# Low parts of the attention's weight sets by ScalarE's negated high part and an accumulating DMA, and reordering copies that run in the order of what they write

## The chip, the cores and the metric

The kernel runs on one core of a Trainium2 chip. The time is device microseconds from launch to end; a run gives one number per execution, and the median of several is compared. In the profile PE is TensorE's matmul and PEld its weight load, DVE is VectorE, ACT is ScalarE, POOL is GpSimd, SP is SyncE, which here issues most of the DMAs.

## What is computed

A trunk of two encoder layers on 512 tokens of width 1024, in float32. Each layer projects x, runs two attentions on the projections (mixer A: windowed, with a learned sink; mixer B: three groups of heads with windows of stride 1, 4 and 16, mixed by their softmax denominators), projects and gates both branches, and ends with two layer norms and a squared-ReLU MLP. Cut to what matters here:

```python
def _mixer_sublayer(x, cos, sin, w_in, b_gate, a_sink, w_branch_a, w_branch_b, w_out):
    proj = jnp.einsum('bsd,de->bse', x, w_in)
    qa, ka, va, qb, kb, vb, gl = jnp.split(proj, IN_SPLITS, axis=-1)
    ...
    oa, _ = _banded_attention(qa, ka, va, A_WINDOW, a_sink)
    ya = jnp.einsum('bse,ed->bsd', oa.reshape(bsz, seq, A_Q_W), w_branch_a)
    ...
    for g, (window, dil) in enumerate(B_GROUPS):      # ((128, 1), (512, 4), (2048, 16))
        o, lse = _dilated_attention(qb[:, :, hs], kb[:, :, hs], vb[:, :, hs], window, dil)
    ...
    yb = jnp.einsum('bse,ed->bsd', ob.reshape(bsz, seq, B_OUT_W), w_branch_b)
    return jnp.einsum('bsd,de->bse', ga * ya + gb * yb, w_out)
```

## The kernel before

Float32 products are made from float32r parts: an operand w is split into a high part hi = round(w) and a low part lo = w − hi, and a product takes three matmuls, hi·hi, lo·hi and hi·lo (`mm3`, lines 279 to 281: the third is the first that reads the low part of the weights). The splits are work for other engines than PE.

Weights arrive in sets of 128 x 1024: `fetch` (L248, DMA from SP into "wst", three buffers) and `prep`, which splits the set into "whi" and "wlo" (three buffers each). `weights(key)` takes the next set of a plan and, with LOOK = 2, makes `prep` of the set two places ahead. So the cast of set c+2 runs as soon as PE has left set c−1, whose buffers it takes, and the set is wanted when PE begins c+2. There are two ways to split. `split` casts on ACT (L227) and subtracts on DVE (L228). `split_later` casts on ACT (L232), writes −hi into the low part on ACT (L233), and lets a DMA issued by POOL add w to it (L234). Which one a set gets is decided by its membership in the tuple LATER; before the change that is only ("ple", 1, 0) of layer 0 and ("start", 0) of layer 1. One activation operand, "pl", is made by `split_later` as well (three such splits in all, around 750 to 765 us).

The attention of a layer (`attention_block`) runs a list FLOW of projections (two "qa", eight "g" gates, and for two head pairs sp and three groups g the sets "qb", "kb", "vb"; four sets "ba" of the branch projection), 24 matmuls for each projection, and puts the attention units (scores, softmax, transposes, weighted sums) between them. The order on PE is made when the program is recorded: a class `Forecast` keeps estimated times of ACT, DVE and POOL, and a unit's next step is taken when the forecast says that its operands are there; otherwise a matmul of a projection goes in. The forecast charges each prep to ACT and DVE by fixed costs, before and after the change alike. The order on ACT, DVE, POOL and SP is set by a scheduler. On the chip each engine runs its list in order and waits where an operand is late. PSUM has one bank "o" for weighted sums; a join (L447 on ACT, L448 on DVE) has to empty it before the next begins.

For groups 1 and 2, tokens are sorted by residue class. `natural` and `sigma` are two views of the same 512 columns: the first in token order, the second in sorted order. `rope` writes the split q and k of these groups through `sigma` (the cast "qh" on L227, the subtraction "ql" on L228), and `values` copies v out of PSUM through it (L392).

Of the kernel before, what the change touches and what calls it, by code (L numbers as in the profile page):

```python
# [24 lines left out]
DEPTH = 2  # L25
# [3 lines left out]
LN_EPS = 1e-5  # L29
ROPE_THETA = 500000.0  # L30
NEG = -3.0e38
LATER = ((0, ("ple", 1, 0)), (1, ("start", 0)))
LOOK = 2
WARM = 11
FLOW = [("qa", 2), ("g", 0), ("qa", 3), ("g", 1), ("b", 0, 0), ("g", 2), ("b", 0, 1), ("b", 0, 2), ("g", 3),
# [165 lines left out]
def build(nc, tc, plan, down, xT, xN, pT, wst, vec, rows, sink, cst, out):  # L201
# [3 lines left out]
    with ctx:  # L205
# [4 lines left out]
        def bank(tag, name):  # L210
            return pp.tile([P, 512], F32, tag=tag, name=name, bufs={"mm": 3, "s": 2, "pt": 2, "o": 1}[tag])
# [14 lines left out]
        def split(hi, lo, src):  # L226
            nc.scalar.copy(hi, src)  # L227
            nc.vector.tensor_tensor(lo, src, hi.bitcast(F32), ALU.subtract)  # L228
# [22 lines left out]
        def prep(c):  # L251
# [3 lines left out]
            for a in cuts:  # L255
                (split_later if plan[c][0] in LATER else split)(hi[:, a], lo[:, a], st[:, a])
            ready[c] = (hi, lo)
# [90 lines left out]
        def attention_block(l, av, rp, vt, OA, OB, begun):  # L348
# [8 lines left out]
                if not l:  # L357
                    nc.sync.dma_start(ident, cst[:, off:])

            def natural(ap):  # L360
                return ap.rearrange("p (a b c) -> p a b c", a=32, b=4)

            def sigma(ap):
                return ap.rearrange("p (c b a) -> p a b c", c=4, b=4)

            def forecast_split(n, after):
                h = fc.on("act", 0.05 + n / 1200, after + HOP)
                return h, fc.on("dve", 0.07 + n / 960, h + HOP)

            def rope(ps, dil, name):  # L370
                sw = av.tile([P, S], F32, tag="sw", name="sw" + name, bufs=2)
                t1 = av.tile([P, S], F32, tag="t1", name="t1" + name, bufs=2)
                nc.vector.stream_shuffle(sw, ps, SWAP)
                nc.vector.tensor_tensor(t1, ps, cc["cos"], ALU.mult)
                nc.gpsimd.tensor_tensor(sw, sw, cc["sin"], ALU.mult)
                nc.vector.tensor_tensor(t1, t1, sw, ALU.add)
                hi = av.tile([P, S], F32R, tag="qh", name="qh" + name, bufs=5)
                lo = av.tile([P, S], F32R, tag="ql", name="ql" + name, bufs=5)
                if dil:
                    split(sigma(hi), sigma(lo), natural(t1))  # L380
                else:
                    split(hi, lo, t1)
                a = fc.on("dve", 0.6, fc.t + HOP)
                b = fc.on("dve", 0.6, a)
                c = fc.on("pool", 1.23, a + HOP)
                fc.give("mm", b + HOP)
                return hi, lo, forecast_split(S, fc.on("dve", 0.6, max(b, c) + HOP))[1] + HOP

            def values(ps, kind, name):
                v = av.tile([P, S], F32, tag="vT", name="vT" + name, bufs=2)  # L390
                if kind == "sigma":
                    nc.scalar.copy(sigma(v), natural(ps))  # L392
                elif kind == "edge":
                    nc.scalar.copy(v[:, 0:64], ps[:, 448:512])
                    nc.scalar.copy(v[:, 64:128], ps[:, 0:64])
                    nc.scalar.copy(v[:, 128:512], ps[:, 64:448])
                else:
                    nc.scalar.copy(v, ps)
                t = fc.on("act", 0.5, fc.t + HOP) + HOP
                fc.give("mm", t)  # L400
                return v, t
# [152 lines left out]
            def unit_b(sp, g, st):  # L554
# [76 lines left out]
                for n, (s, ms) in enumerate(groups):  # L631
                    pT = done[n]
                    if g or n % 2 == 0:
                        yield lambda: fc.t >= max(pT[2], t_v) and fc.open("o")
                        fc.take("o")
                        o = bank("o", f"o{nm_}_{s}")
                    else:
                        yield lambda: fc.t >= pT[2]
                    if ms:
                        for i, m in enumerate(ms):  # L640
                            dst = o[:, (m - 1) * P:(m + 1) * P] if m else \
                                o.rearrange("p (j t) -> p j t", j=4)[:, ::3, :]
                            weighted(dst, v, m, s, pT, slice(i * 256, (i + 1) * 256), m == 1, m == 0)
                        fc.pe(0.43)
                        if n % 2:
                            t_f = join(f, o, s)
                    else:
                        for c in range(4):
                            cs = slice(c * P, (c + 1) * P)
                            for m, (a, b) in enumerate(PASSES):  # L650
                                nc.tensor.matmul(o[:64, cs], v[:, c, s, a, :], pT[b][:, cs], start=m == 0, stop=m == 2)
                        fc.pe(0.64)
                        nc.scalar.copy(natural(f[s * 64:s * 64 + 64, :]), sigma(o[:64, :]))
                        t_f = fc.on("act", 0.48, fc.t + HOP) + HOP
                        fc.give("o", t_f)
                    fc.give("pT", fc.t)
                    if n + 2 < len(groups):
                        yield able(n + 2)
                        transposed(n + 2)
# [63 lines left out]
            fc.take("mm")  # L723
            fc.take("mm")
            held["ka"] = rope(kps, False, f"ka{l}")
            va, t_va = values(vps, "natural", f"va{l}")
            fc.take("mm")
            fc.take("s", 3.5)
            held["qa", 0] = rope(q0, False, f"qa{l}_0")
            fc.take("mm")  # L730
            held["qa", 1] = rope(q1, False, f"qa{l}_1")
            side = []

# [17 lines left out]
            def filler():  # L751
# [6 lines left out]
                for kind, *idx in FLOW:  # L758
                    if kind == "qa":
                        yield from project(("qa", *idx), False)  # L760
                    elif kind == "b":
                        yield from project(("qb", *idx), idx[1] > 0)
                        yield from project(("kb", *idx), idx[1] > 0)
                        ps = yield from steps((l, ("vb", *idx)), X)
                        nm_ = "vb" + "_".join(str(v) for v in (l, *idx))
                        v, t = values(ps, "sigma" if idx[1] else "edge", nm_)
                        side.append([v_unit(("vb", *idx), v, t, nm_), None])
                    elif kind == "g":
                        ps = yield from steps((l, ("g", 0, *idx)), X)
                        ga.append(gate(l, 0, idx[0], vt, rp, ps))  # L770
                        fc.give("mm", fc.on("act", 0.57, fc.t + HOP) + HOP)
                    else:
                        yield lambda: not any(k[0] == "a" for k in (*waiting, *live))
                        u = idx[0]
                        w = weights((l, ("ba", u)))
                        fc.on("dve", 1.135, fc.on("act", 0.947, fc.t + HOP) + HOP)
                        for n, g in enumerate(ga[2 * u:2 * u + 2]):
                            yield lambda: fc.open("mm")
                            ps = bank("mm", f"ya{l}_{u}_{n}")
                            fc.take("mm")  # L780
                            for i in range(4):
                                mm3(ps, w, n * 4 + i, OA[i], i == 0, i == 3)
                                fc.pe(0.645)
                                yield None
                            nc.vector.scalar_tensor_tensor(g, g, 1.0, ps, ALU.add, ALU.mult)
                            fc.give("mm", fc.on("dve", 0.6, fc.t + HOP) + HOP)
# [258 lines left out]
        begun, ple = None, {}  # L1045
# [12 lines left out]
        for l in range(DEPTH):  # L1058
# [33 lines left out]
            for u in range(4):  # L1092
                gs = [gate(l, 1, t, vt, rp) for t in (2 * u, 2 * u + 1)]
                w = weights((l, ("bb", u)))
                for n, g in enumerate(gs):
                    t = 2 * u + n
                    ps = bank("mm", f"yb{l}_{t}")
# [49 lines left out]
            with tc.manual_schedule(engines={PE}):  # L1147
# [10 lines left out]
                for a in range(4):  # L1158
                    ahead(at[0] + a)
                    ps = bank("mm", f"wo{l}_1_{a}")  # L1160
# [34 lines left out]
            with tc.manual_schedule(engines={PE}):  # L1195
                for q in range(FQ):
                    for i, m in enumerate(UP_ORDER):
# [3 lines left out]
                        ps = bank("mm", f"ps_up{l}_{q}_{m}")  # L1201
# [163 lines left out]
```

## Time and profile before

| | |
|---|---|
| median of 3 runs | 1545.58 us (1545.32 to 1548.82) |
| the profiled execution | 1545.51 us |
| its span, first to last instruction | 1543.7 us |
| granted TensorE clock | 0.996 |
| instructions in the span | 19566 |
| DMA | 162.19 MB, mean 105 GB/s |
| weight fetches wst<-wst, issue to landing | 3.5 us median, 512 KB each |

The attention of layer 0 lies between about 28 and 258 us of the span, that of layer 1 between about 797 and 1027. A wait is put down in the profile to the instruction whose semaphore came last; "idle before" is the time in which an engine had nothing to run. Matmuls are pipelined, and where one ends is modelled.

### The profile page before, as it was taken

The numbers are of one execution on the slowest core, as the hardware profiler recorded it, in microseconds if no ns is written. First come the engines' busy times: TensorE is split into PE (matmuls) and PEld (weight loads), VectorE is DVE, ScalarE is ACT, GpSimd is POOL, SyncE is SP. The second block draws the span as 40 slices with busy tenths as digits, with TensorE's granted clock in tenths as the row PEclk, the third lists the DMA queues.
The fourth block names the chain that finished last, engine by engine and source line by source line (L and its number), as shares of the span: only waits on it lengthen the run. The fifth ranks groups of instructions, "written<-read, shape, count | busy, mean of one in ns | idle before, by whom it ended". The sixth has DMA issues, their size and how long they took to land.

```text
span 1543.7 us, 19566 instructions
## 1 busy us (share of the span) xinstructions
PE 1516.1 (98%) x7438; PEld 1244.0 (81%) x7438; DVE 1089.2 (71%) x1803; ACT 717.4 (46%) x1192; POOL 205.4 (13%) x161
## 2 busy tenths in 40 slices
PE   9999999999999999999999999999999999999996
PEld 7778788888888888888887778888888888888885
DVE  6778675467568767696877786744575776767868
ACT  4566554344334443434546665542442443444343
POOL 1011110020011120202010101111100211111022
PEclk9999999999999999999999999999999999999998
DMA  6211224244612415142342121254446233241403
GB/s 219 69 55 55 69 69 170 84 131 158 199 65 83 146 45 162 43 149 70 96 149 69 55 68 56 80 164 146 136 136 211 68 99 120 70 135 55 150 1 96
DMA packets 46461, 162.19 MB, mean 105 GB/s; under 512 B 5664, under 2 KB 6048, under 8 KB 46368
## 3 DMA queue, kind: packets, MB, share of 16 engines
q1 hardware_dynamic: 43200, 151.74, 29.3%
q0 software_dynamic: 2448, 8.91, 3.0%
q8 instruction: 58, 0.95, 0.2%
q10 hardware_dynamic: 720, 0.30, 0.1%
q14 instruction: 35, 0.29, 0.1%
HBM read 155.16 MB, written 4.19 MB: 103 GB/s over the span
## 4 chain that ended last, share of the span: by engine, by line
PE 87%; DVE 8%; ACT 2%; issue 1%; DMA 1%; ACTq 0%; SPq 0%; DVEq 0%
PE dn L1017 16%; PE ps_up L280 8%; PE ps_up L279 8%; PE ps_up L281 8%; PE pg L287 2%; PE wo L285 2%; PE wo L287 2%; PE wo L286 2%; PE pg L286 2%; PE pg L285 2%; DVE wlo L228 2%; PE sa L438 1%; PE pta L416 1%; PE ya L279 1%; PE ya L281 1%
## 5 line engine op out<-in xcount | busy, mean ns | idle before, releaser
L228 DVE TENSOR_TENSOR wlo<-wst,whi 128x1024 fp32r<-128x1024 f32 (+1 forms) x172 | 220.7, 1286 | 150.9 <-ACT whi L227 144.3
L227 ACT CAST whi<-wst 128x1024 fp32r<-128x1024 f32 (+1 forms) x172 | 175.7, 1022 | 299.5 <-PE ps_up L280 115.5
L279 PE MATMUL ps_up<-xhi,whi 128*128 128x512 f32 x512 | 199.2, 389 | 0.0
L280 PE MATMUL ps_up<-xlo,whi 128*128 128x512 f32 x512 | 199.2, 389 | 0.0
L281 PE MATMUL ps_up<-xhi,wlo 128*128 128x512 f32 x512 | 199.2, 389 | 0.0
L990 POOL TENSOR_TENSOR hr<-r 128x512 f32<-128x512 f32 x64 | 102.2, 1597 | 551.4 <-ACT r L982 530.9
L279 PEld LDWEIGHTS ps_up<-xhi,whi 128*128 128x128 f32 x512 | 96.1, 188 | 20.0
L281 PEld LDWEIGHTS ps_up<-xhi,wlo 128*128 128x128 f32 x512 | 96.1, 188 | 20.0
L280 PEld LDWEIGHTS ps_up<-xlo,whi 128*128 128x128 f32 x512 | 96.1, 188 | 19.8
L227 ACT CAST whi<-raw 128x1024 fp32r<-128x1024 f32 x56 | 58.0, 1053 | 97.0 <-PE ps_up L280 64.1
L227 ACT CAST dhi<-raw 128x1024 fp32r<-128x1024 f32 x56 | 58.7, 1051 | 82.2 <-PE dn L1017 59.8
L1036 DVE TENSOR_TENSOR y<-y,dn 128x512 f32<-128x512 f32 x96 | 65.2, 681 | 38.5 <-PE dn L1017 38.5
L970 DVE TENSOR_TENSOR raw<-raw,raw 128x1024 f32<-128x1024 f32 x64 | 86.4, 1349 | 0.2
L228 DVE TENSOR_TENSOR wlo<-raw,whi 128x1024 fp32r<-128x1024 f32 x56 | 68.1, 1219 | 14.1 <-ACT whi L227 14.1
L228 DVE TENSOR_TENSOR dlo<-raw,dhi 128x1024 fp32r<-128x1024 f32 x56 | 69.2, 1239 | 5.5 <-ACT dhi L227 5.5
L1017 PE MATMUL dn<-whi,smh 128*128 128x512 f32 x128 | 50.1, 394 | 0.7 <-DVE y L1036 0.7
L1017 PE MATMUL dn<-wlo,smh 128*128 128x512 f32 x128 | 50.6, 395 | 0.2
L287 PE MATMUL pg<-bhi,xlo 128*128 128x512 f32 x128 | 49.9, 390 | 0.6 <-DVE xlo L914 0.6
L1017 PE MATMUL dn<-whi,sml 128*128 128x512 f32 x128 | 49.9, 390 | 0.0
L285 PE MATMUL pg<-bhi,xhi 128*128 128x512 f32 x128 | 49.9, 390 | 0.0
L1017 PE MATMUL dn<-dhi,smh 128*128 128x512 f32 x128 | 49.9, 390 | 0.0
L1017 PE MATMUL dn<-dlo,smh 128*128 128x512 f32 x128 | 49.8, 389 | 0.0
(846 smaller groups left out, 3889.0 us busy)
## 6 DMA issues: line engine op xcount, KB each, us to landing
wst<-wst SPq DMA_DIRECT2D x187, 512.0 KB, 3.5
raw<-wst SPq DMA_DIRECT2D x64, 512.0 KB, 4.2
y<-rows POOLq DMA_DIRECT2D x14, 512.0 KB, 7.6
row<-rows SPq DMA_DIRECT2D x7, 512.0 KB, 9.8
wst<-wst SPq DMA_DIRECT2D x9, 256.0 KB, 2.7
xs<-xT SPq DMA_DIRECT2D x8, 256.0 KB, 5.7
y<-xN SPq DMA_DIRECT2D x4, 512.0 KB, 6.9
kept<-y SPq DMA_DIRECT2D x4, 512.0 KB, 2.9
```

Source lines behind the costliest of these rows:

```text
L227: nc.scalar.copy(hi, src)
L228: nc.vector.tensor_tensor(lo, src, hi.bitcast(F32), ALU.subtract)
L279: nc.tensor.matmul(ps, w[0][:, s], x[0], start=start, stop=False, skip_group_check=part)
L280: nc.tensor.matmul(ps, w[0][:, s], x[1], start=False, stop=False, skip_group_check=part)
L281: nc.tensor.matmul(ps, w[1][:, s], x[0], start=False, stop=stop, skip_group_check=part)
L285: nc.tensor.matmul(ps, x[0], w[0][:, c], start=start, stop=False)
L286: nc.tensor.matmul(ps, x[0], w[1][:, c], start=False, stop=False)
L287: nc.tensor.matmul(ps, x[1], w[0][:, c], start=False, stop=stop)
L970: nc.vector.tensor_tensor(to, to, other, ALU.add)
L990: nc.gpsimd.tensor_tensor(h.rearrange("p s t -> p (s t)"), r, r, ALU.mult)
L1017: nc.tensor.matmul(ps[s], a[:, k, tok], w[b][:, cols], start=first and not (k or m), stop=k == 3 and m == 2, skip_group_check=True)
L1036: return nc.vector.tensor_tensor(to, to, ps, ALU.subtract if n in (2, 4, 5) else ALU.add)
```

## The change

LATER now also holds, for both layers, the eight gates of branch 0 and all eighteen "qb", "kb", "vb" sets. `prep` therefore sends these 26 sets per layer through `split_later`: the subtraction on DVE (L228) goes, an activation with scale −1 on ACT (then L234) and an accumulating DMA on POOL (L235) come. The sets "start", "qa", "ba" and everything from the second gates on keep `split`. `natural` and `sigma` get an argument for the order in which a view is walked, and three copies use it: they still move the same elements, but in the order "c b a", in which the written side is contiguous and the read side strided; before, it was the other way round.

```diff
-LATER = ((0, ("ple", 1, 0)), (1, ("start", 0)))
+LATER = ((0, ("ple", 1, 0)), (1, ("start", 0)), *((l, n) for l in range(DEPTH) for n in (
+    *(("g", 0, t) for t in range(8)), *((n, sp, g) for n in ("qb", "kb", "vb") for sp in range(2) for g in range(3)))))
...
-            def natural(ap):
-                return ap.rearrange("p (a b c) -> p a b c", a=32, b=4)
+            def natural(ap, order="a b c"):
+                return ap.rearrange(f"p (a b c) -> p {order}", a=32, b=4)
 
-            def sigma(ap):
-                return ap.rearrange("p (c b a) -> p a b c", c=4, b=4)
+            def sigma(ap, order="a b c"):
+                return ap.rearrange(f"p (c b a) -> p {order}", c=4, b=4)
...
                 if dil:
-                    split(sigma(hi), sigma(lo), natural(t1))
+                    split(sigma(hi, "c b a"), sigma(lo, "c b a"), natural(t1, "c b a"))
...
                 if kind == "sigma":
-                    nc.scalar.copy(sigma(v), natural(ps))
+                    nc.scalar.copy(sigma(v, "c b a"), natural(ps, "c b a"))
```

Lines behind the first diff stand one number later in the changed kernel. The order on PE is the same, row for row. On the other engines it moves, shown here at three places of layer 0.

DVE, in the unit b of head pair 1, group 0, while its probabilities are split (ptlb is the low part of a transposed block, numbered pair, group, block; wlo the low part of a weight set; t_qb, sw_qb and ql_qb belong to the rope of the next q). Before:

```order
L374 TENSOR_TENSOR t_qb_1_2089<-ps_('qb', 1, 1)_2013,ct_157 128x512
L228 TENSOR_TENSOR ptlb_1_0_0_2073<-ptb_1_0_0_2067,pthb_1_0_0_2072 128x512
L228 TENSOR_TENSOR wlo_2101<-wst_2098,whi_2100 128x1024
L228 TENSOR_TENSOR ptlb_1_0_1_2085<-ptb_1_0_1_2079,pthb_1_0_1_2084 128x512
L376 TENSOR_TENSOR t_qb_1_2089<-t_qb_1_2089,sw_qb_1_2088 128x512
L228 TENSOR_TENSOR ptlb_1_0_2_2122<-ptb_1_0_2_2116,pthb_1_0_2_2121 128x512
```

After:

```order
L375 TENSOR_TENSOR t_qb_1_2108<-ps_('qb', 1, 1)_2032,ct_157 128x512
L229 TENSOR_TENSOR ptlb_1_0_0_2092<-ptb_1_0_0_2086,pthb_1_0_0_2091 128x512
L229 TENSOR_TENSOR ptlb_1_0_1_2104<-ptb_1_0_1_2098,pthb_1_0_1_2103 128x512
L377 TENSOR_TENSOR t_qb_1_2108<-t_qb_1_2108,sw_qb_1_2107 128x512
L229 TENSOR_TENSOR ptlb_1_0_2_2142<-ptb_1_0_2_2136,pthb_1_0_2_2141 128x512
```

The subtraction between the two splits is gone, and nothing took its place.

ACT, where the values of head pair 0, group 1 (vTvb_0_1) are copied out for PE to transpose (fa is the join of unit a, ptha a block of its probabilities, pb the exponentials of the next unit). Before:

```order
L447 COPY fa_3_1146<-oa_3_0_1297 64x512
L227 CAST ptha_3_4_1358<-pta_3_4_1354 128x384
L227 CAST whi_1370<-wst_1368 128x1024
L392 COPY vTvb_0_1_1366<-ps_('vb', 0, 1)_1231 128x32x4x4
L427 ACTIVATE pb_0_0_0_1259,cn_0_326<-pb_0_0_0_1259,cn_0_326 128x256
```

After:

```order
L448 COPY fa_3_1155<-oa_3_0_1308 64x512
L228 CAST ptha_3_4_1369<-pta_3_4_1365 128x384
L233 CAST whi_1381<-wst_1379 128x1024
L393 COPY vTvb_0_1_1377<-ps_('vb', 0, 1)_1242 128x512
L234 ACTIVATE wlo_1382<-whi_1381 128x1024
L428 ACTIVATE pb_0_0_0_1270,cn_0_327<-pb_0_0_0_1270,cn_0_327 128x256
```

The copy keeps its place behind the cast and now writes 512 contiguous columns; the negated high part comes behind it and ahead of the exponentials.

POOL, over the first projections of mixer B (sw is the rope's product with the sines, of q or k). Before:

```order
L375 TENSOR_TENSOR sw_qa_496<-sw_qa_496,ct_157 128x512
L375 TENSOR_TENSOR sw_qb_0_717<-sw_qb_0_717,ct_157 128x512
L375 TENSOR_TENSOR sw_kb_0_798<-sw_kb_0_798,ct_157 128x512
L563 MEMSET pb_0_0_0_1259 128x64
L564 MEMSET pb_0_0_0_1259 128x64
```

After:

```order
L376 TENSOR_TENSOR sw_qa_499<-sw_qa_499,ct_157 128x512
L235 DMA wlo_512<-wst_509 128x1024
L235 DMA wlo_633<-wst_630 128x1024
L376 TENSOR_TENSOR sw_qb_0_722<-sw_qb_0_722,ct_157 128x512
L235 DMA wlo_735<-wst_732 128x1024
L376 TENSOR_TENSOR sw_kb_0_804<-sw_kb_0_804,ct_157 128x512
L235 DMA wlo_817<-wst_814 128x1024
L235 DMA wlo_923<-wst_920 128x1024
L235 DMA wlo_1040<-wst_1037 128x1024
```

Accumulating DMAs now stand between the rope's products, each behind the wait for its negated high part on ACT. On SP, a weight buffer is refilled only when the accumulating DMA that reads it has landed, and at the end of each attention one fetch stands behind the first two loads of y instead of ahead of them.

## The prediction

> **What bounds the kernel now.** I read the busy times first, then the stages (busy time of each engine in a stretch), then who makes PE wait. PE is busy for 98% of the span of 1543.7 us:
>
> ```profile
> PE 1516.1 (98%) x7438; PEld 1244.0 (81%) x7438; DVE 1089.2 (71%) x1803; ACT 717.4 (46%) x1192; POOL 205.4 (13%) x161
> ```
>
> The instructions on PE and their order are the same before and after, so the change can only move the 27.6 us in which PE is idle (1543.7 − 1516.1), and only in the two attention stages, where it acts. Those stages are these stretches; the columns are start:end, length, then busy time and count of PE, PEld, DVE, ACT, POOL, clock, DMA share, GB/s:
>
> ```profile
> 28.00:258.00 230.00, 224.85 (x1333) 181.90 (x1333) 171.80 (x419) 135.23 (x311) 27.55 (x27) 1.00 0.20 66
> 797.00:1027.00 230.00, 224.84 (x1333) 181.92 (x1332) 171.77 (x419) 135.35 (x311) 27.55 (x27) 1.00 0.20 65
> ```
>
> PE idles 230.00 − 224.85 = 5.15 us in a stage, 10.3 in both. The stages are twins, so I work one out and double it. DVE, busy for 171.8 of 230, is the most loaded engine beside PE. The waits of PE (total in us, times, longest) that lie in these stages:
>
> ```profile
> PE vtvb L406 <- ACT vTvb L392: 3.1, 2, 1.6
> PE pta L416 <- ACT pa L427: 2.2, 4, 0.7
> PE ob L443 <- DVE ptlb L228: 1.6, 2, 0.8
> PE ob L651 <- DVE ogb L448: 1.5, 2, 0.8
> PE rs L461 <- ACT wide L455: 1.5, 4, 0.4
> ```
>
> They add up to 9.9 us: these are all that can be won, seven waits in each layer.
>
> **The change part by part.** Of the 32 weight sets of each layer's attention flow, 26 (8 gates, 18 q/k/v) give up the subtraction on DVE and get a negative copy on ACT and an accumulating DMA from POOL. In one stage the removed and the reordered work is:
>
> ```profile
> L228 DVE TENSOR_TENSOR wlo<-wst,whi 128x1024 fp32r<-128x1024 f32 x28 | 39.9, 1424 | 8.0 <-ACT whi L227 6.2 <-PE sb L438 1.5
> ...
> L227 ACT CAST qh_kb<-t_kb 128x512 fp32r<-128x512 f32 x6 | 5.8, 962 | 7.1 <-DVE t_kb L376 7.1
> ...
> L447 ACT COPY fa<-oa 64x512 f32<-64x512 f32 x8 | 4.7, 581 | 1.4 <-PE oa L443 1.1
> L653 ACT COPY ogb<-ob 64x512 f32<-64x512 f32 x8 | 4.6, 579 | 7.2 <-PE ob L651 7.0
> ```
>
> 25 of these 28 subtractions go (the 26th, of gate 0, runs before 28 us; one "qa" and two "ba" sets keep theirs): 25 × 1.424 = 35.6 us off DVE per stage, 172 to 136. What comes instead has three samples already, at the end of layer 0, where three operand pairs are split this way:
>
> ```profile
> L232 ACT CAST whi<-wst x2: 1037/1046/1056, 754.3 to 762.3; 128x1024 fp32r<-128x1024 f32 x2
> ```
> ```profile
> L233 ACT ACTIVATE wlo<-whi x2: 1062/1062/1063, 755.4 to 763.4; 128x1024 fp32r<-128x1024 f32 x2
> ```
> ```profile
> L234 POOL DMA_DIRECT2D wlo<-wst x2: 862/866/870, 756.8 to 764.8; - x2
> ...
> DMA to landing us min/median/max: 4.6/5.0/6.5
> ```
>
> So ACT gets 25 × 1.06 = 26.5 us more and POOL 25 × 0.87 = 21.7 (27.6 to 49). The low part is there about 2.5 + 5.0 = 7.5 us after its cast begins (cast 754.3, issue 756.8, landing), and up to 2.5 + 6.5 = 9.0. Before it took cast plus subtraction, 1.05 + 1.42.
>
> Four waits hang from a subtraction that goes. First, before unit a(0)'s transposes:
>
> ```profile
> 51.22 1.21 DVE L228 TENSOR_TENSOR wlo<-wst,whi 128x1024 fp32r<-128x1024 f32 x1
> ...
> 53.65 0.15 DVE L492 SCALAR_TENSOR_TENSOR nma<-mxa,nsk 128x2 f32<-128x2 f32 x1
> ...
> 54.29 0.51 ACT L427 ACTIVATE pa<-pa,nma 128x256 f32<-128x256 f32 x1
> ...
> 54.94 0.20 PEld L416 LDWEIGHTS pta<-ident,pa 128*128 128x128 f32 x2 [0.91 <-ACT pa L427]
> 54.94 0.33 PE L416 MATMUL pta<-ident,pa 128*128 128x128 f32 x1 [0.67 <-ACT pa L427]
> ```
>
> The maxima behind the subtraction, the bias "nma" and the exponential start 1.21 us earlier, more than the 0.67 that PE waits. The other pair of pta waits is shorter, and the exponential there moves ahead of a cast on ACT. I take 2.0 of 2.2. Second, the split of transposed probabilities shown in the order above:
>
> ```profile
> 194.93 1.43 DVE L228 TENSOR_TENSOR wlo<-wst,whi 128x1024 fp32r<-128x1024 f32 x1
> ...
> 196.28 0.68 DVE L228 TENSOR_TENSOR ptlb<-ptb,pthb 128x512 fp32r<-128x512 f32 x1
> ...
> 197.02 0.33 PE L443 MATMUL ob<-ptlb,vvvb 128*64 128x256 f32 x1 [0.82 <-DVE ptlb L228]
> ```
>
> The split came straight behind the subtraction; without it, it runs 1.43 us earlier, before PE gets there, and all 1.6 goes. Third, the join that frees the only "o" bank:
>
> ```profile
> 153.01 1.22 DVE L228 TENSOR_TENSOR wlo<-wst,whi 128x1024 fp32r<-128x1024 f32 x1
> ...
> 153.58 0.58 ACT L447 COPY ogb<-ob 64x512 f32<-64x512 f32 x1
> ...
> 154.25 0.69 DVE L448 TENSOR_TENSOR ogb<-ob,ogb 64x512 f32<-64x512 f32 x1
> ...
> 155.00 0.27 PE L651 MATMUL ob<-pthb,vvvb 128*64 128x128 f32 x1 [0.76 <-DVE ogb L448]
> ```
>
> Here ACT's half of the join ends at 154.16, so what is late next is ACT, and only its own earlier start helps (shorter reordering copies, earlier exponentials, less one negative copy). I take 1.1 of 1.5. Fourth, the token scaling of unit m:
>
> ```profile
> 247.22 1.23 DVE L228 TENSOR_TENSOR wlo<-wst,whi 128x1024 fp32r<-128x1024 f32 x1 [0.84 <-ACT whi L227]
> ...
> 250.82 0.44 PE L461 MATMUL rs<-ident,wide 128*128 128x128 f32 x2 [0.44 <-ACT wide L455]
> ```
>
> The subtraction stands among the small DVE steps that end in "wide"; ACT's negative copy now sits between the exponential and "wide", while DVE does those steps. I take 1.2 of 1.5.
>
> The fifth wait hangs from a reordering copy itself:
>
> ```profile
> 128.43 1.05 ACT L392 COPY vTvb<-ps_('vb', 0, 1)_1231 128x512 f32<-128x512 f32 x1
> ...
> 129.54 0.33 PE L406 MATMUL vtvb<-ident,vTvb 128*128 128x128 f32 x1 [1.56 <-ACT vTvb L392]
> ```
>
> A copy that writes contiguously and reads PSUM in strides stands in the trace: L653, 579 ns, no more than the contiguous L447 with 581. So the new form lies between 0.58 (a contiguous copy is the floor) and today's 1.05; I take 0.58, the row of the same kind: 0.47 × 2 = 0.9 of 3.1. The same holds for the q and k casts and their DVE halves; they are hidden behind PE's projections and count nothing.
>
> The Trainium skill, "SBUF — State Buffer", section "Door 1: The DMA port swizzle", speaks against this: every access that crosses into a new line (16 bytes in SBUF, 8 in PSUM) pays, so strides moved to the read side would cost as they did on the write side, and this term would be 0. By L653, which reads PSUM in strides and pays nothing, the trace does not agree; strided reads of SBUF no row shows.
>
> Sum: 2.0 + 1.6 + 1.1 + 1.2 + 0.9 = 6.8 us. The view counts idle time from a modelled end of the matmul before; the weight load of the same transposes shows 0.91 where the matmul shows 0.67. I add a fifth: 8.2.
>
> Against it stand the new waits, which the trace does not show. On ACT: behind each negative copy are queued casts of transposed probabilities, exponentials and joins. At the nearest rows the waits that ACT ends (pta, vtvb, rs) are five per stage; each lengthened by a whole 1.06 is 5.3 per stage, 10.6 in all, the upper end; the lower is 0, where ACT idles (it is busy 135 of 230 us, then 135 + 26.5 − 6 = 156, the 6 being twelve reordering copies at about 0.5). Most of the copies stand in front of such idle time, so I take 1.0. On PE, behind a low part that lands late: nothing while the 7.5 to 9.0 us fit between the cast and the first matmul that reads the low part. Over the 26 sets of layer 0 this lead is 11.8 us at the first and 12.3 at the last, and longer at all others:
>
> ```profile
> 23.49 1.05 ACT L227 CAST whi<-wst 128x1024 fp32r<-128x1024 f32 x1 [2.52 <-PE ps_start L280]
> ```
> ```profile
> 35.31 0.39 PE L281 MATMUL ps_('g', 0, 0)_387<-xhi,wlo 128*128 128x512 f32 x1
> ```
> ```profile
> 252.68 1.05 ACT L227 CAST whi<-wst 128x1024 fp32r<-128x1024 f32 x1 [0.49 <-PE ya L280]
> ```
> ```profile
> 264.99 0.39 PE L281 MATMUL ps_('g', 0, 7)_2759<-xhi,wlo 128*128 128x512 f32 x1
> ```
>
> On POOL the rope multiplications (L375) now queue behind DMA issues of 0.87 us, which wait for ACT; the issues of a set stand behind the rope of the set before, so both come about together, and I count 0. On SP a weight buffer comes free some 6 us later, and one fetch moves behind two loads of y; the fetch is needed a set or more later: 0.
>
> Net 8.2 − 1.0 = 7.2. The profiled execution took 1545.51 us (the median of the three is 1545.58): 1545.5 − 7.2 = **1538.3 us**.
>
> **The rivals.** (A) Low parts land late, slower. The longest landing of an accumulating DMA on POOL, among the fourteen of L923 (y<-rows), is 14.0 us:
>
> ```profile
> DMA to landing us min/median/max: 4.9/7.6/14.0
> ```
>
> With 2.5 + 14.0 = 16.5 gate 0 is late by 4.7 us and gate 7 by 4.2, 8.9 per layer, 17.8 in all: 1538.3 + 17.8 = 1556.1. It decides from a landing of 11.8 − 2.5 = 9.3 us on. Against it: those 14.0 us stand among four loads of y and four such DMAs at once, while attention uses the DMA engines for 0.20 of the time; the three DMAs of the same kind took 4.6 to 6.5. A reason why they might take long is whether DVE holds up their issue; beside DVE work with two SBUF operands the issue took as long as elsewhere:
>
> ```profile
> 752.67 1.22 DVE L228 TENSOR_TENSOR wlo<-raw,whi 128x1024 fp32r<-128x1024 f32 x1
> 753.11 0.88 POOL L234 DMA_DIRECT2D pl<-pf  x1 [22.88 <-ACT pl L233]
> ```
>
> That DVE shuts GpSimd out of the descriptors of its own DMAs is a rule of the Trainium skill ("SBUF — State Buffer", section "SBUF: two separate sides"); it would give this rival's time, and 0.88 against 0.87 does not bear it out. (B) ACT becomes the bound: the upper end above, 10.6 in place of 1.0, gives 1547.9. For it speaks that ACT works almost without a gap from 145 to 154 us; against it, that it had first waited 1.66 us for maxima on DVE there, which now come earlier:
>
> ```profile
> 144.81 0.41 ACT L427 ACTIVATE pb<-pb,cs 128x128 f32<-128x128 f32 x1 [1.66 <-DVE cs L602]
> ```
>
> (C) The reordered copies are no faster: 0.9 × 1.2 = 1.1 less, 1539.4. (D) All 9.9 goes, times 1.2: 1533.6.
>
> **How the numbers follow.** Forecast 0.56, A 0.09, B 0.22, C 0.08, D 0.05. The range goes from D into B's upper end, 1533 to 1549; A and the fringes are left out. What a measurement can tell from no change is 0.3%, 4.6 us. Faster than 1540.9: the forecast (but 0.04 of it), C, D and a little of B, 0.66; slower than 1550.2: A, 0.09; the rest, 0.25.
>
> **What would show it.** Right: PE's waits on ptlb, on the join and on rs gone, vtvb's under 2.4 in all, "vTvb" and the four strided "qh" casts near 0.6 us, DVE at 132 to 137 of 230 and ACT near 156, no PE wait on a DMA into wlo. Wrong: PE waits on wlo in L281 (A), PE waits on ACT that are longer or new (B), reordering copies of 1.05 us or more (C).

## The result and the profile after

| | before | after |
|---|---|---|
| median | 1546.07 us (4 runs, 1545.32 to 1548.82) | 1537.97 us (4 runs, 1535.22 to 1539.62) |
| ratio, 95% interval | | 0.9947 [0.9935, 0.996] |
| profiled execution, its span | 1545.51, 1543.7 us | 1536.4, 1534.6 us |

The changed kernel is 8.1 us faster (6 to 10 by the interval). The busy times of its page, to be laid beside the first row that the prediction shows:

```profile
PE 1512.5 (99%) x7438; PEld 1243.0 (81%) x7438; DVE 1017.7 (66%) x1751; ACT 763.7 (50%) x1244; POOL 246.4 (16%) x213
```

The two attention stages (start:end, length, busy time and count of PE, PEld, DVE, ACT, POOL, clock, DMA share, GB/s); they now end some 6 us earlier, so 225 us are shown in place of 230:

```profile
28.00:253.00 225.00, 224.56 (x1339) 182.75 (x1338) 138.70 (x395) 157.56 (x336) 47.16 (x52) 1.00 0.53 127
793.00:1018.00 225.00, 224.56 (x1337) 182.78 (x1336) 138.34 (x393) 157.38 (x336) 45.68 (x52) 1.00 0.52 127
```

PE idles 0.44 us in a stage where it idled 5.15. What PE waits for in the whole program after the change (total us, times, longest):

```profile
PE ya L280 <- ACT gate L847: 1.9, 1, 1.9
PE dn L1018 <- DVE y L1037: 1.7, 5, 0.4
PE pg L288 <- DVE xlo L915: 1.2, 1, 1.2
PE warm L222 <- DVE rgap L218: 1.0, 1, 1.0
PE ps_start L280 <- ACT xhi L228: 1.0, 1, 1.0
PE ps_start L280 <- ACT whi L228: 0.6, 1, 0.6
PE rs L462 <- ACT wide L456: 0.4, 2, 0.2
```

Of the five waits of the prediction only 0.4 us on rs is left, and behind the attention there is one that before did not have: ya on "gate" (ps_start on "xhi", new as well, stands at the start of the program). Since PE's instructions and their order are the same, each can be compared with itself: the start of the n-th matmul after, less its start before. This lead (negative where the changed kernel is ahead) changes almost only in steps, and the steps say where time was won or lost, without any modelled end. The large ones (us):

| where (start before, layer 0) | step, layer 0 | step, layer 1 |
|---|---|---|
| pta, 54.94 | −0.83 | −0.83 |
| pta, 111.15 | −0.60 | −0.60 |
| vtvb, 129.54 | −1.72 | −1.72 |
| ob behind the join, 155.00 | −0.70 | −0.70 |
| rs, 180.10 and 250.82 | −0.44, −0.24 | −0.45, −0.24 |
| ob behind ptlb, 197.02 | −0.98 | −0.98 |
| the whole flow, 36.9 to 253 and 797 to 1022 | **−6.32** | **−6.39** |
| behind it, 1022 to 1052 | | **+2.26** |
| all other stages together | +1.16 | |

So the attention flow became 12.7 us shorter (11.0 in the steps listed, 1.7 in small ones), 2.3 were given back right behind it in layer 1, and 1.2 lie in other stages, at the start and at four waits on DVE. At the last matmul that makes 9.3 us; the two spans differ by 9.1. In the runs below these other stages come out between −0.5 and +1.3 without an edit there, so I don't explain them.

**The largest step, vtvb.** ACT and DVE of the kernel before, ahead of it:

```profile
116.47 2.02 DVE L228 TENSOR_TENSOR wlo<-wst,whi 128x1024 fp32r<-128x1024 f32 x1
...
123.83 0.17 DVE L584 TENSOR_SCALAR cn<-mxb 128x4 f32<-128x4 f32 x1
...
124.03 0.46 ACT L427 ACTIVATE pb<-pb,cn 128x192 f32<-128x192 f32 x1 [1.37 <-DVE cn L584]
```

And after:

```profile
121.15 0.15 DVE L585 TENSOR_SCALAR cn<-mxb 128x4 f32<-128x4 f32 x1
...
121.34 0.46 ACT L428 ACTIVATE pb<-pb,cn 128x192 f32<-128x192 f32 x1 [0.84 <-DVE cn L585]
...
125.74 0.58 ACT L393 COPY vTvb<-ps_('vb', 0, 1)_1242 128x512 f32<-128x512 f32 x1
```

From the first exponential (pb) to the v copy ACT works without a gap, 4.40 us in both kernels (124.03 to 128.43; 121.34 to 125.74). The exponentials start 2.69 us earlier, PE at that place only 1.34: a gain of 1.35 us on PE, from DVE. The copy itself, 1.05 to 0.58, gives 0.47 more, and both together cover the step of 1.72.

**The new wait.** Behind layer 1's attention, on SP and on ACT of the changed kernel (ph is the high part of pf, an operand of a later stage):

```profile
1012.04 0.86 SPq L1081 DMA_DIRECT2D y<-kept  x2
1021.71 0.33 SPq L249 DMA_DIRECT2D wst<-wst  x1
1022.09 0.97 SPq L1081 DMA_DIRECT2D y<-kept  x2
1023.11 0.47 SPq L1112 DMA_DIRECT2D pf<-pT  x1
```
```profile
1031.81 1.05 ACT L228 CAST ph<-pf 128x1024 fp32r<-128x1024 f32 x1 [8.75 <-DMA pf<-pT]
1032.76 1.04 ACT L228 CAST whi<-wst 128x1024 fp32r<-128x1024 f32 x1
1033.71 0.68 ACT L847 ACTIVATE gate<-ps_('g', 0, 7)_9300,vhalf 128x512 f32<-128x512 f32 x1
```

And before, where PE was at this place 12.2 us later:

```profile
1024.88 1.87 SPq L1080 DMA_DIRECT2D y<-kept  x4
1026.79 0.47 SPq L1111 DMA_DIRECT2D pf<-pT  x1
```
```profile
1036.98 1.05 ACT L227 CAST ph<-pf 128x1024 fp32r<-128x1024 f32 x1 [1.74 <-DMA pf<-pT]
```

There the four loads of y went out together and pf behind them; ACT waited 1.74 us for it, and no one for ACT. Now a fetch stands in the middle, and it waits until 1021.71 for a weight buffer. The last adding DMA of the flow, gate 7's, is issued at 1012.52 and takes 9.1 us to land, the longest of its kind: 1021.66. The fetch waits for that landing, because the adding DMA reads the buffer. Two loads of y and pf queue behind the fetch, ACT waits 8.75 us for pf, gate 7's activation queues behind ACT's wait, and PE needs the bank that it empties.

### The profile page after: what moved, and what is told of

The parts are those of the page before. It is cut to its first block, busy times and chain, and to the rows that moved or that the text cites. A ratio compares the mean times of both kernels' runs of the same rounds, so it can differ in the third digit from the quotient of the medians.

```text
span 1534.6 us, 19685 instructions
## 1 busy us (share of the span) xinstructions
PE 1512.5 (99%) x7438; PEld 1243.0 (81%) x7438; DVE 1017.7 (66%) x1751; ACT 763.7 (50%) x1244; POOL 246.4 (16%) x213
## 4 chain that ended last, share of the span: by engine, by line
PE 88%; DVE 5%; DMA 3%; ACT 2%; issue 1%; POOL 0%; SPq 0%; POOLq 0%; DVEq 0%; ACTq 0%
PE dn L1018 16%; PE ps_up L281 8%; PE ps_up L280 8%; PE ps_up L282 8%; PE pg L288 2%; PE wo L288 2%; PE wo L287 2%; PE wo L286 2%; PE pg L286 2%; PE pg L287 2%; PE sa L439 1%; PE pta L417 1%; DMA raw<-wst 1%; PE sb L439 1%; PE ps_start L281 1%
## 5 line engine op out<-in xcount | busy, mean ns | idle before, releaser
L228 ACT CAST whi<-wst 128x1024 fp32r<-128x1024 f32 (+2 forms) x120 | 121.2, 1010 | 257.8 <-PE ps_up L281 115.5
L229 DVE TENSOR_TENSOR wlo<-wst,whi 128x1024 fp32r<-128x1024 f32 (+2 forms) x120 | 145.5, 1216 | 128.2 <-ACT whi L228 127.4
L228 ACT CAST whi<-raw 128x1024 fp32r<-128x1024 f32 x56 | 58.0, 1053 | 97.0 <-PE ps_up L281 57.7
L228 ACT CAST dhi<-raw 128x1024 fp32r<-128x1024 f32 x56 | 58.7, 1052 | 82.2 <-PE dn L1018 60.1
L235 POOL DMA_DIRECT2D wlo<-wst x54 | 47.4, 877 | 244.8 <-ACT wlo L234 157.6
L233 ACT CAST whi<-wst 128x1024 fp32r<-128x1024 f32 x54 | 56.7, 1051 | 42.5 <-PE ps_start L281 6.9
L234 ACT ACTIVATE wlo<-whi 128x1024 fp32r<-128x1024 f32 x54 | 57.3, 1061 | 0.9
```

## The experiments

All are compared with the kernel before, run on the same chip. "Flow" and "behind" are the steps of the table above, summed over both layers (us).

| kernel | median | ratio, 95% interval | flow | behind |
|---|---|---|---|---|
| changed kernel | 1537.97 | 0.9947 [0.9935, 0.996] | −12.7 | +2.3 |
| e1 low parts only | 1540.81 | 0.9962 [0.9949, 0.9976] | −10.7 | +5.9 |
| e2 copies only | 1543.72 | 0.9983 [0.9974, 0.9992] | −1.9 | 0.0 |
| e3 without gate 7 | 1533.17 | 0.9912 [0.9899, 0.9926] | −12.8 | 0.0 |
| e4 five sets | 1536.92 | 0.9936 [0.9924, 0.9949] | −8.9 | 0.0 |
| e5 pf from ACT | 1534.36 | 0.9923 [0.9909, 0.9936] | −12.8 | +1.2 |
| e6 POOL subtracts | 1558.38 | 1.0078 [1.0065, 1.0092] | +12.8 | 0.0 |
| e7 negated twice | 1538.89 | 0.9952 [0.994, 0.9965] | −6.9 | 0.0 |
| e8 eight sets | 1536.10 | 0.9933 [0.992, 0.9945] | −10.4 | 0.0 |
| e9 no low part | 1535.41 | 0.9929 [0.9915, 0.9943] | −11.2 | 0.0 |

**e1 and e2: the two parts apart.** e1 leaves `natural`, `sigma` and the copies as before; e2 leaves LATER as before.

> Low parts as in the changed kernel, the three reordering copies as before. Theory (the subtractions stood in front of the chains that PE waits for, the copy out of PSUM adds 0.47 us at one place per layer): PE's waits on pta, ptlb, join and rs stay gone, the wait on vtvb comes back with some 0.5 us in each layer, so about 1 us more than the changed kernel, near 1539, and 7 less than before. Rival (the reordering copies carry the gain, since vtvb with 1.72 us per layer is the largest piece of it): 3.4 us more than the changed kernel, near 1541.5.

> Reordering copies as in the changed kernel, all low parts but the three of before by subtraction on DVE. Theory: the v copy takes 0.58 us in place of 1.05, vtvb's wait falls by 0.5 us in each layer and the other waits stay, so 1 us less than before, near 1545. Rival (the copies carry the gain): 3.4 us less, near 1542.5. The q and k casts and their subtractions stay above 1.0 us.

The two add up: 10.7 + 1.9 = 12.6 of 12.7 in the flow. The vtvb step is −1.25 in e1, −0.69 in e2 and −1.72 with both edits, so e1 lacks about half a microsecond there in each layer; the second half microsecond that it lacks is at the join at 155, where ACT's half comes straight behind a v copy. So by the flow the copies are worth 2.0 us, twice the theory's 1 and well short of the rival's 3.4. The medians alone would not decide it: e2's lies 2.9 lower than before, and its interval, 1.2 to 4.0, leaves the theory's 1 out and holds the rival's 3.4. e1's 1540.81 is nearer to the rival's time as well, 2.8 slower than the changed kernel and so more than its 2.0 in the flow; the trace shows why, since what comes behind is dearer there: ACT waits 10.9 us for pf and PE 4.0 us for the gate.

```profile
1032.61 0.39 PE L282 MATMUL ya<-oah,wlo 128*128 128x512 f32 x1
1036.95 0.80 PE L280 MATMUL ya<-oah,whi 128*128 128x512 f32 x1 [3.95 <-ACT gate L847]
1037.54 0.63 PE L281 MATMUL ya<-oal,whi 128*128 128x512 f32 x1
```

**e3 and e5: the loss behind the flow.** e3 gives gate 7 back to the subtraction; e5 keeps the adding DMA and moves one load.

```diff
 e3
-    *(("g", 0, t) for t in range(8)), ...
+    *(("g", 0, t) for t in range(7)), ...
 e5
-            nc.sync.dma_start(pf, pT[l])
+            nc.scalar.dma_start(pf, pT[l])
```

> The changed kernel with the last gate of the flow, (g, 0, 7) of both layers, split by subtraction again. Theory (the 2.1 us that PE loses at the end of layer 1's attention come from the last accumulating DMA: its weight buffer comes free late, the fetch that waits for it stands on SP ahead of the last two loads of y and of pf, and ACT waits for pf): pf lands some 8 us earlier, ACT's wait for pf and PE's wait on ACT's gate (1.9 us) go, 2 us less than the changed kernel, near 1536. Rival (pf is late because the loads of y and the adding DMAs fill the DMA engines anyway): pf lands as late, PE's wait on gate stays, no change.

> The changed kernel, but the load of pf is issued by ACT and no longer stands on SP behind the fetch that waits for gate 7's weight buffer. The adding DMA of gate 7, the loads of y and their adding DMAs stay. Theory (order on SP): in layer 1 pf is issued near 1014 us in place of 1023.1 and lands some 9 us later, before 1025; ACT's wait of 8.8 us for it and PE's wait of 1.9 us on the gate go, 2 us less than the changed kernel, near 1536. Rival (the DMA engines are full from 1020 to 1034 anyway): pf lands near 1031 all the same, no change.

e3, on SP and ACT, at the same place:

```profile
1011.70 2.31 SPq L1081 DMA_DIRECT2D y<-kept  x4
1014.05 0.93 SPq L1112 DMA_DIRECT2D pf<-pT  x1
```
```profile
1023.16 1.05 ACT L228 CAST ph<-pf 128x1024 fp32r<-128x1024 f32 x1 [1.09 <-DMA pf<-pT]
```

pf goes out 9 us earlier and is there 9 us later (before it took 10); PE's wait on the gate is gone and nothing is lost behind the flow. In e5 the same holds with the adding DMA and the late loads of y still there: pf goes out at 1012.71, ph begins at 1022.30, and no PE wait on the gate is left. So it was the order on SP, not full DMA engines. But e5 has a wait of its own:

```profile
1020.77 0.39 PE L281 MATMUL ps_('g', 0, 7)_9300<-xlo,whi 128*128 128x512 f32 x1
1022.05 0.50 PE L282 MATMUL ps_('g', 0, 7)_9300<-xhi,wlo 128*128 128x512 f32 x1 [0.89 <-DMA wlo<-wst]
```
```profile
DMA to landing us min/median/max: 4.5/4.6/10.4
```

With one more load beside it gate 7's adding DMA took 10.4 us, and PE waited for a low part. The step there is 1.05 us. In layer 0 of e5 the landing took 9.5 us and the step is 0.20; at 9.1 us (changed kernel) and 9.3 (e1) there is no step. In the changed kernel the low part lands at 1021.66 and is read at 1021.90. e3 is the best kernel of all, 4.8 us below the changed one by the medians and 3.3 by the two traces, where 2 were expected. Where the other 1.5 lie is open: two of the changed kernel's four runs have a span of 1537.8 us and no trace; a dearer wait behind the flow, as in e1, could explain them, but no run shows it.

**e4 and e8: load or position.** Only the sets whose subtraction stood in front of a waiting chain are changed, five or eight of each layer:

```diff
 e4
+    ("kb", 0, 0), ("kb", 0, 2), ("kb", 1, 0), ("qb", 1, 2), ("g", 0, 6)
 e8
+    ("kb", 0, 0), ("qb", 0, 2), ("kb", 0, 2), ("kb", 1, 0), ("qb", 1, 1), ("kb", 1, 1), ("qb", 1, 2), ("g", 0, 6)
```

> Reordering copies as in the changed kernel, but only five sets of each layer without the subtraction: kb(0,0), kb(0,2), kb(1,0), qb(1,2) and gate 6, whose subtractions ran ahead of the unit's maxima at 51, of the maxima at 116, of the join at 153, of ptlb's split at 195 and among the steps of rs at 247 us. Theory (single subtractions at the wrong place cost, not DVE's load): of the 6.3 us that attention got shorter in each layer 4 to 5.5 stay, and nothing is lost at the end of layer 1, so 8 to 11 us less than before, 1535 to 1538. Rival (DVE's load as a whole sets the waits): 5 of 26 parts of the gain and the copy's 1 us, 3.4 less than before, near 1542.5.

> The kernel with five sets (1536.9 us) and three more without the subtraction: qb(0,2), qb(1,1) and kb(1,1), which stood near the second pta wait (0.60 us per layer) and in front of the steps that end in rs at 180 us (0.45; the subtraction at 172.4 took 1.93 us). Theory (single subtractions): both steps go in both layers, 2.1 us less, near 1534.8, within 1 us of the kernel with 25 sets and no gate 7 (1533.2), with 16 of its 50 sets. Rival (DVE's load as a whole): what the other 20 sets brought (3.7 us) is shared evenly, three of them bring 0.6, near 1536.3.

e4, the first stage:

```profile
28.00:253.00 225.00, 223.81 (x1331) 181.42 (x1330) 163.86 (x413) 138.03 (x316) 32.12 (x32) 1.00 0.26 77
```

DVE is still busy for 163.9 of 225 us, and 8.9 of the 12.7 us are there. About 2 of the 8.9 are the copies' (e2); the five sets of each layer bring the other 7, of the 10.7 that 26 sets bring in e1: position, not load. Of the three sets more, e8's flow wins 1.5 us: rs at 180 goes as expected (0.45 in each layer), but the second pta wait does not move, so 1.2 of the theory's 2.1 us fail to come. The median, 1536.10, is the rival's 1536.3 and not the theory's 1534.8, so that by the time alone the rival would stand; what speaks against it is the trace, where the gain stands at single places: 0.9 us at rs, which e4 does not have. Why pta stays is shown with e9.

**e9: what the new way costs.** The 26 sets get no low part at all.

```diff
+            if free:
+                nc.scalar.copy(hi[:, a], st[:, a])
+                ready[c] = (hi, hi)
+                return
```

> The changed kernel without any low part for the 26 sets of each layer: no subtraction, no negated copy, no adding DMA; the third matmul of each product reads the high part a second time, so the output is not the reference's. It prices what the new way of making low parts costs. Theory (the negated copies lie beside PE's work, and what the new way costs is the 2.1 us at the end of layer 1 and the last pieces of the join at 155 and of rs at 251 us, 0.6 per layer): 1 to 2 us less than the kernel without gate 7's low part by DMA (1533.2 us), near 1532. Rival (the first negated copy costs like the second one did, 5.7 us): near 1527.5. If the copies cost nothing at all: 1533.

Its flow is not shorter than the changed kernel's, but 1.5 us longer, 1.2 of it at the second pta, 0.60 in each layer; at 1535.41 us it is 2.2 slower than e3. So the negated copies and the adding DMAs cost the flow nothing that can be seen, and neither expectation hit. The second pta hangs on ACT's order. ACT of e9, and then of the changed kernel:

```profile
109.54 0.48 ACT L228 CAST ptha<-pta 128x384 fp32r<-128x384 f32 x1 [1.86 <-PE pta L424]
109.92 0.51 ACT L435 ACTIVATE pa<-pa,nma 128x256 f32<-128x256 f32 x1
```
```profile
107.62 1.06 ACT L234 ACTIVATE wlo<-whi 128x1024 fp32r<-128x1024 f32 x1
109.13 0.51 ACT L428 ACTIVATE pa<-pa,nma 128x256 f32<-128x256 f32 x1 [0.45 <-DVE nma L493]
```

In e9, as in e8 and before, the exponentials stand behind a cast that waits for PE. In the changed kernel the scheduler put the exponentials in front, as a by-product of the other changes; no subtraction was in the way. In e8 and before, the bias "nma" had been ready 0.9 us ahead of the exponentials, so there the order on ACT alone holds them. In e9 the bias is late too: its step on DVE begins beside a POOL product, takes 0.95 us in place of 0.15 and ends at 109.76, only 0.16 ahead of the exponentials.

**e7: a second negated copy.** The edit doubles one line of e3.

```diff
             nc.scalar.activation(lo, hi.bitcast(F32), AF.Copy, scale=-1.0)
+            nc.scalar.activation(lo, hi.bitcast(F32), AF.Copy, scale=-1.0)
```

> The kernel without gate 7's low part by DMA (1533.2 us), with the negated copy written twice: ACT gets a second 1.06 us for each of 25 sets in each layer, and is then busy for some 184 of 225 us. The product is the same. Theory (most copies stand in ACT's idle time): 0 to 2 us more, 1533 to 1535. Rival (ACT is near its limit; each copy delays what PE waits for): up to 10 us more, 1540 to 1544. With it the low parts are there 1.06 us later, 8.6 to 10.1 us after the cast begins, against a lead of 11.8 us: no wait on wlo.

5.7 us more than e3, 5.9 in the flow: too much for the theory, and at 1538.89 short of the rival's 1540 to 1544. The stage and two waits:

```profile
28.00:253.00 225.00, 222.23 (x1325) 180.05 (x1324) 138.82 (x393) 178.10 (x358) 47.09 (x52) 1.00 0.51 122
```
```profile
PE ob L653 <- DVE ogb L450: 2.5, 2, 1.2
...
PE pta L418 <- ACT pa L429: 1.5, 4, 0.5
```

ACT is busy for 178 of 225 us, not the 184 that I expected, as the stage got longer. The join and pta come back, where ACT works without gaps. The first copy of each set cost nothing that e9 can show, the second did: what an engine has left in a whole stage says little of what it has left at one place.

**e6: POOL does the subtraction.**

```diff
-            nc.scalar.activation(lo, hi.bitcast(F32), AF.Copy, scale=-1.0)
-            nc.gpsimd.dma_start(lo, src, accum_op=ALU.add)
+            nc.gpsimd.tensor_tensor(lo, src, hi.bitcast(F32), ALU.subtract)
```

> The changed kernel, but POOL subtracts the low part itself; neither a negated copy on ACT nor an adding DMA. At 1.6 us for a 128x512 product of POOL such a subtraction takes some 3.2 us; the low part is there 4.3 us after the cast begins and the weight buffer is free then, so that the end of layer 1 loses nothing. Theory (only what stands on DVE ahead of the chains counts): all of the gain stays, 1534 to 1536. Rival (DVE slows down beside POOL: the subtraction at 172.4 us, beside a product of POOL, took 1.93 us in place of 1.22): 80 us of POOL work in each layer lengthen the DVE steps beside them by up to a half, PE's waits on DVE come back, 1540 to 1547.

Slower than before, and by more than the rival said. The groups of the first stage, and then one pair of rows from the timelines:

```profile
L234 POOL TENSOR_TENSOR wlo<-wst,whi 128x1024 fp32r<-128x1024 f32 x24 | 57.6, 2400 | 78.6 <-ACT whi L233 77.0 <-PE ob L443 1.7
...
L376 DVE TENSOR_TENSOR t_kb<-t_kb,sw_kb 128x512 f32<-128x512 f32 x6 | 14.9, 2479 | 3.5 <-POOL sw_kb L375 3.5
```

The same group before:

```profile
L376 DVE TENSOR_TENSOR t_kb<-t_kb,sw_kb 128x512 f32<-128x512 f32 x6 | 4.1, 680 | 0.9 <-POOL sw_kb L375 0.9
```

The pair of rows, POOL and DVE:

```profile
118.40 2.38 POOL L234 TENSOR_TENSOR wlo<-wst,whi 128x1024 fp32r<-128x1024 f32 x1
```
```profile
118.48 2.85 DVE L376 TENSOR_TENSOR t_kb<-t_kb,sw_kb 128x512 f32<-128x512 f32 x1 [0.83 <-POOL sw_kb L375]
```

The rope's sum, 0.68 us before, waits for POOL's product and so starts just when POOL begins the subtraction; it ends 0.55 us behind POOL's end. It is not slower by up to a half, as the rival had it, but held until POOL is done. The waits that this makes, rs above all (+2.83 in each layer at 182), are new ones. Of the prediction's waits the first pta at 55, ptlb at 197 and the join at 155 go in e6 as well; the second pta is 0.8 us longer, and of vtvb's step only 0.47 of 1.72 is there.

## Why the prediction was right, step by step

Forecast 1538.3, measured 1537.97 (8.1 us less by the medians, 9.3 at the last matmul of the two traces): the likeliest case came in, and most of its mechanism with it. That the numbers agree so closely is luck: vtvb and SP were wrong by 2.3 us each, with opposite signs, and small steps, ACT and the other stages nearly cancel too.

| step | predicted, times 1.2 | measured |
|---|---|---|
| pta | 2.4 | 2.9 |
| ptlb | 1.9 | 2.0 |
| join | 1.3 | 1.4 |
| rs | 1.4 | 1.4 |
| vtvb | 1.1 | **3.4** |
| small steps, not counted | 0 | 1.7 |
| new waits on ACT | −1.0 | 0 |
| SP | 0 | **−2.3** |
| other stages | 0 | −1.2 |
| sum | 7.2 | 9.3 |

**pta, ptlb, join, rs.** Sizes and reasons held, with one exception: the second pta moved by ACT's order, which the prediction named ("the exponential there moves ahead of a cast on ACT") without seeing that before the change this alone held it (e8). At the join ACT's half was late next, as said, and the shorter v copy in front of it gave half a microsecond per layer (e1).

**vtvb: a term mis-sized.** I took only the copy, "0.47 × 2 = 0.9 of 3.1", and overlooked that the same ACT chain began with exponentials that waited 1.37 us for DVE, behind a subtraction of 2.02 us. By e1, 1.25 of the 1.72 are the low parts, and the copy has the rest.

**The copies.** "vTvb" takes 0.58 to 0.60 us, as taken. "The four strided qh casts near 0.6" was wrong: six casts of k in a stage, of which two are not strided, before and after (ns, minimum/median/maximum):

```profile
L227 ACT CAST qh_kb<-t_kb x6: 618/1122/1147, 81.8 to 228.2; 128x512 fp32r<-128x512 f32 x6
```
```profile
L228 ACT CAST qh_kb<-t_kb x6: 620/1086/1102, 78.9 to 221.6; 128x512 fp32r<-128x512 f32 x6
```

Rival C was thus half right: reading SBUF in strides costs nearly what writing it did. It changed nothing, since those casts are hidden. The rule weighed there (the Trainium skill, "SBUF — State Buffer", section "Door 1: The DMA port swizzle") agrees with these 1.09 us for SBUF. For PSUM the Trainium skill speaks there of matmuls alone, and ACT's copy out of PSUM, with its 0.58 us, pays nothing.

**Load.** DVE at 138.7 of 225 lies just above the "132 to 137" of 230, part of it because the reordered subtractions of q and k stayed near 1.06 us; ACT at 157.6 answers to "near 156". The gain did not come from the load (e4).

**Rival B** (ACT becomes the bound): the first copies cost nothing that can be seen (e9); a second copy of each set cost 5.7 (e7), about half of the rival's 10.6.

**Rival A** (late low parts): the threshold was right, partly by luck. It "decides from a landing of 9.3 us on": 9.1 and 9.3 did no harm, 9.5 cost 0.20 us and 10.4 cost 1.05 (e5). That 9.3 was worked out for gate 0; gate 7, which it now concerns, has the longer lead of 12.3 us but its DMA is issued 2.9 us behind the cast (1009.59 to 1012.52) and not 2.5. Only this one set per layer comes near it; the median landing is 4.6. The issue did not slow down beside DVE (0.85 to 0.90 us but for one of 1.01). The Trainium skill states the lock-out weighed there for a DVE step in a 2-port perf mode ("SBUF — State Buffer", section "SBUF: two separate sides"); whether the subtraction of the prediction's row is one, no run here shows.

**SP: the step that failed.** "One fetch moves behind two loads of y; the fetch is needed a set or more later: 0." I asked when the fetch is needed and not what then stands behind the fetch while it waits for its buffer: two loads of y and pf. That cost 2.3 us (e3, e5). Without it the kernel stands at 1533.2 (e3), close to rival D's 1533.6: nearly all of the waits did go, with 0.44 us of idle PE left in a stage.

## What to carry to other kernels

A long operation of no urgency on an in-order engine costs where it stands ahead of a waiting chain, not by its share of the load; moving a few such operations to an idle engine can bring most of the gain. When a change frees a buffer later, look at the queue in which the next load waits for that buffer, and price everything behind it there. An asynchronous step that lands in time at the median is decided by its slowest landing, and that is found where other transfers start: leave the last one of a stage on the short way.

## What the runs showed of the hardware

- A DVE step with two SBUF operands that begins inside a POOL step of the kind is held until that one has ended: 2.85 us in place of 0.68 (e6). It was so already before. In layer 0's attention nine subtractions of a weight set began 0.33 to 0.94 us into a POOL product; they took 1.43 to 2.03 us in place of 1.22, and all ended 1.08 us behind the product. The one of 2.02 us above is among them (the product runs from 116.14 to 117.42). One more, at 109.45, was not held; there the POOL product took 2.76 us in place of 1.28. A DVE product that reads PSUM beside POOL kept its 0.69 us (217.84). The Trainium skill states this as a lock held for a whole instruction ("SBUF — State Buffer", section "SBUF: two separate sides"); the rows agree.
- PE's clock after an idle stretch: 1.95 us of waiting left it at 1.00 (changed kernel), and behind 3.95 us it fell to 0.50 (e1). Granted clock is the third column from the right:

```profile
1034.00:1036.00 2.00, 0.00 (x0) 0.00 (x0) 0.60 (x1) 1.68 (x2) 0.27 (x1) 1.00 1.02 419
1036.00:1038.00 2.00, 1.05 (x3) 0.86 (x4) 2.00 (x3) 1.42 (x3) 0.00 (x0) 0.70 1.12 286
1038.00:1040.00 2.00, 2.00 (x6) 1.63 (x5) 2.00 (x3) 0.53 (x1) 0.00 (x0) 0.50 1.03 231
1040.00:1042.00 2.00, 2.00 (x9) 1.58 (x9) 0.57 (x2) 0.00 (x0) 0.00 (x0) 0.94 1.04 232
```

  The slow matmuls behind it (0.63 us long in place of 0.39) add 5.9 − 4.1 = 1.8 us to a step of 4.1. The Trainium skill has the clock halved after an idle window of about 3.4 us ("TensorE: Matmul & The Clock Gate", section "What's actually happening"), which fits both.
- An accumulating DMA of 512 KB within SBUF landed in 4.6 us at the median, and in 8.3 to 10.4 for gate 7's, issued within 1.6 us behind a fetch and two loads of y (changed kernel, e1, e5).
